# Products of ones at the start, first weights loaded in pieces, input squares as side work, and later places for the decays and the delta rule's sums, in a two-layer decoder trunk

## The chip, the core and the metric

One core of a Trainium2 chip runs the whole program. TensorE (PE, with its weight loads, PEld) multiplies, VectorE (DVE), ScalarE (ACT) and GpSimd (POOL) do the elementwise work, SyncE (SP) issues nearly all DMAs. The metric is the device time of one execution in microseconds (us); lower is better. The kernel before takes 2602.82 us, the median of three runs (2601.01 to 2603.27).

## The reference

The input is x, 256 positions of 2048 features in float32. Two layers follow one another; each adds a mixer, a cross-attention to a memory and a convolutional feed-forward block to the residual stream, each on an RMS-normalized input. The change lies in the mixer of the first (even) layer, which joins stick-breaking attention with a gated delta rule:

```python
def rmsnorm(x, g):
    y = xf * lax.rsqrt(jnp.mean(xf * xf, axis=-1, keepdims=True) + EPS)
    return (y * g.astype(jnp.float32)).astype(x.dtype)

def even_mixer(h, w_in, sconv_w, a_log, dt_bias, gdn_norm, w_out):
    sb_q, sb_k, sb_v, gdn_qkv, gdn_a, gdn_b, gdn_gate = split_cols(h @ w_in, [...])
    o_a = merge_heads(stick_breaking_attention(...))
    gq, gk, gv = split_cols(jax.nn.silu(causal_dwconv(gdn_qkv, sconv_w)), [...])
    log_decay = -jnp.exp(a_log) * jax.nn.softplus(gdn_a + dt_bias)
    beta = jax.nn.sigmoid(gdn_b)
    o_b = gated_delta_rule(l2norm(gq heads), l2norm(gk heads), gv heads, log_decay, beta)
    o_b = rmsnorm(o_b, gdn_norm) * jax.nn.silu(gdn_gate heads)
    return jnp.concatenate([o_a, o_b], axis=-1) @ w_out
```

There are eight delta-rule heads of width 128, worked in chunks of 64 positions.

## The kernel before

The residual stream stays on chip, features on partitions: X[0] to X[15], 128x256 each, loaded as eight tiles of two. Every float32 product is made of rounded parts: a weight slab (`raw`, 128x1024, 512 KB, five buffers) becomes `hi`, a rounded copy made by ACT (L229), and `lo`, the rest, made by DVE in two halves of 512 columns (L232); four pairs of such buffers are kept. An input tile X[k] becomes `xs`, 128x512, whose left half ACT writes (L218) and whose right half DVE writes (L219). One step of a matrix product (`mm_tile`) is then a product of `hi` with all 512 columns of `xs` (L261) and one of `lo` with the left 256 (L262), called a pair below; 16 pairs make one 128-wide output column block, `gemm`.

Work that is not a weight product, the attention chains and the delta rule, is written as generators. `Side` runs them between pairs: each pair is one tick, and `yield n` asks for at least n ticks before the generator goes on. A scheduler then moves single instructions a little; on each engine they execute strictly in the order that it leaves.

`even()` starts with the head of the program: for each k, X[k] is split into `xs`, multiplied with the first key weights of the delta rule (g0), and, from k = 4 on, with a narrow weight `wab` for the decays (`decay_products`, L437, two products into `pab`). GpSimd squares the odd X[k] and adds them up (L360, L364, `Norm.square`); the even ones are squared by ACT and added by DVE (L353, L354, `Norm.add`). The sums of both accumulators over partitions (L372) give the norm R, first wanted when the first three gemms of the delta rule are done. The generator `decays` turns `pab` into g, beta and their cumulated forms: two transposes on TensorE (L481), a chain of small ACT and DVE instructions, 12 ticks, then four small products (L499). For every two heads `delta_pair` normalizes keys and queries: squares (ACT writes the rounded square L566, GpSimd squares again L567 and subtracts L568), 8 ticks, sums over partitions on TensorE (L551), a reciprocal root (`rsqrt`, from L327) and the scaled `kq`, first for keys, then the same for queries, then 17 ticks before the products of `kq` (L585). Near its end the same is done for its output (ACT L713, L714, GpSimd L715), 8 ticks before the sums.

The weight slabs come from SP's queue in the order of use; the head's DMAs are in a list, `order`, that starts with the first X tile, the first slab of 512 KB, the second X tile and `wab`.

Of the kernel before, what the change touches and what calls it, by code (L numbers as in the profile page):

```python
# [10 lines left out]
F32 = mybir.dt.float32  # L11
F32R = mybir.dt.float32r
I32 = mybir.dt.int32
AF = mybir.ActivationFunctionType
# [133 lines left out]
def build(tc, nc, a):  # L148
# [23 lines left out]


    A.preload_act_table_set("natural_log_exp_and_others")
    cg = cp.tile([P, NCOL + 256], F32, name="cg")
# [3 lines left out]
    nc.scalar.dma_start(cg[:, 0:n0], a["cg"][:, 0:n0])  # L179
    order = [("x", 0), ("w", 0), ("x", 1), ("ab", 0), ("x", 2), ("x", 3), ("x", 4), ("w", 1), ("x", 5), ("x", 6), ("x", 7), ("q", 0), ("cg", 0), ("q", 1)]  # L180
    early = {}
    for what, j in order:
        if what == "x":
            nc.sync.dma_start(XT[j], a["x"][:, 2 * j:2 * j + 2])
        elif what == "cg":
            nc.sync.dma_start(cg[:, n0:], a["cg"][:, n0:])
        else:
            early[what, j] = load(a["wab"] if what == "ab" else a["w"][2 * OFF["ev_gq" if what == "q" else "ev_gk"] + j])
# [15 lines left out]
    def acc(name="a"):  # L204
        return pa.tile([P, 512], F32, name="ps_" + name, tag=name)
# [4 lines left out]
    def f32(ap):  # L210
        return ap.bitcast(F32)
# [12 lines left out]
    def part(raw):  # L224

        n = raw.shape[-1]
        hi = wp.tile([P, 1024], F32R, name="hi", bufs=4)
        lo = wp.tile([P, 1024], F32R, name="lo", bufs=4)
        A.copy(hi[:, 0:n], raw)  # L229
        for h in range(2):  # L230
            s = slice(h * n // 2, (h + 1) * n // 2)
            V.tensor_tensor(out=lo[:, s], in0=raw[:, s], in1=f32(hi[:, s]), op=ALU.subtract)  # L232
        return hi, lo

    cache = {}
# [190 lines left out]
    def even():  # L426
# [12 lines left out]
        for k in range(KD):  # L439
            first.feed(k, False)  # L440
            if k == 0:
                cache[OFF["ev_gk"], 0] = part(early["w", 0])
            if k == 2:
                wab = [e(f"wab{i}", (P, 512), 2, F32R, "kq0") for i in range(2)]
                A.copy(wab[0], early["ab", 0])
                V.tensor_tensor(out=wab[1], in0=early["ab", 0], in1=f32(wab[0]), op=ALU.subtract)
            if k == 7:
                cache[OFF["ev_gk"], 1] = part(early["w", 1])
            mm_tile(g0, [(OFF["ev_gk"], k, k)], xs, first=k == 0, last=k == KD - 1)
            if k >= 4:  # L450
                decay_products(k - 4)
            if k % 2:
                nm.square(X[k], G)
        for k in range(KD - 4, KD):
            decay_products(k)
        for k in range(0, KD, 2):
            nm.add(X[k], V)
            if k % 8 == 0:
                cache[OFF["ev_gq"], k // 8] = part(early["q", k // 8])
        mix, vts = [None] * 16, [None] * 2  # L460
# [12 lines left out]
        def decays():  # L473
            nc.sync.dma_start(cev, a["cev"][:, 0:3 * P])
            nc.sync.dma_start(cst, a["cev"][:, 3 * P:10 * P])
            nc.sync.dma_start(strict, a["iev"])
            y = evac(pab, 32)
            times(y[0:32], y[0:32], nm.R[0:32])
            ab = acc()
            for t in range(2):  # L480
# [13 lines left out]
            V.tensor_scalar(out=nbt, in0=bt, scalar1=-1.0, scalar2=None, op0=ALU.mult)  # L494
            yield 12
            g2 = g.rearrange("p t h -> p (t h)")
# [47 lines left out]

        def squares():
            return tmp("sq", bufs=2), e("sqs", (P, 2, S), 2, F32R, "sbs")

# [6 lines left out]
        def delta_pair(h0, kq0s, vs, sgts):  # L554
# [5 lines left out]
            vec = lambda n: e(n, (P, 2, P), 2)  # L560
            kq = [e("kq", (P, 2, 2, P), 2) for _ in two]
            for q in range(2):
                sps = []
                for i in two:
                    sq, sp = squares()
                    A.activation(sp[:, 0], kq0s[i][:, q], AF.Square)  # L566
                    G.tensor_tensor(out=sq, in0=kq0s[i][:, q], in1=kq0s[i][:, q], op=ALU.mult)  # L567
                    G.tensor_tensor(out=sp[:, 1], in0=sq, in1=f32(sp[:, 0]), op=ALU.subtract)  # L568
                    sps.append(sp)
                yield 8  # L570
                for i in two:
                    ps = sum_squares(sps[i])
                    r = rsqrt(ps, 256, 1.0).rearrange("p (t n) -> p t n", t=2)
                    z = kq0s[i][:, q].rearrange("p (t n) -> p t n", t=2)
                    V.scalar_tensor_tensor(out=kq[i][:, :, q], in0=z, scalar=P ** -0.5 if q else 1.0, in1=r, op0=ALU.mult, op1=ALU.mult)
            yield 17

# [103 lines left out]
            for c in range(4):  # L681
# [27 lines left out]
                yield 4  # L709
            sps = []  # L710
            for i in two:
                sq, sp = squares()
                A.activation(sq, po[:, i * 256:i * 256 + 256], AF.Square)  # L713
                A.copy(sp[:, 0], sq)  # L714
                G.tensor_tensor(out=sp[:, 1], in0=sq, in1=f32(sp[:, 0]), op=ALU.subtract)  # L715
                sps.append(sp)
            yield 8
            for i in two:
# [640 lines left out]
```

## Time and profile before

| what | value |
|---|---|
| median of three runs | 2602.82 us |
| the profiled execution's own time | 2601.66 us |
| its span, first to last instruction | 2599.9 us |
| TensorE busy | 2562.2 us (99%) |
| VectorE busy | 1983.2 us (76%) |
| ScalarE busy | 1480.6 us (57%) |
| GpSimd busy | 197.5 us (8%) |
| mean granted TensorE clock | 0.998 |

All times inside the program count from the start of the span. A bracket behind an instruction names how long its engine sat idle before it and what released it. Ends of TensorE products are modelled, so that a busy share of 99% does not mean full throughput; starts are what to compare.

### The profile page before, as it was taken

To read this page: it belongs to the slowest core of one execution; us is meant where nothing else is said; L and a number is where in the kernel's file an instruction comes from. 1 tells how busy PE (TensorE), PEld (TensorE's weight loads), DVE (VectorE), ACT (ScalarE), POOL (GpSimd) and SP (SyncE) were. 2 spreads that over 40 slices of the span, in tenths; PEclk is the share of its full clock that TensorE was granted. 3 is DMA by queue.
4 is the path that set the end of the run, shared out by engine and by line. 5 is a ranking of instruction groups with operands and counts; after the bars stand their busy time and mean duration, and the time that the engine had idled before them with its cause. 6 is when DMAs were issued, how large, how long until landed. Compare 5 with 4: busy or idle time off the path is not lost.

```text
span 2599.9 us, 41291 instructions
## 1 busy us (share of the span) xinstructions
PE 2562.2 (99%) x15183; PEld 2227.8 (86%) x15183; DVE 1983.2 (76%) x4045; ACT 1480.6 (57%) x2496; POOL 197.5 (8%) x267
## 2 busy tenths in 40 slices
PE   8999999999999999999999999999999999999997
PEld 6887888888888888888888888888988888888886
DVE  7888866877877767767777777886877777777766
ACT  6777655646655545545456555754655545545544
POOL 2111100201000000000011012120200000000001
PEclk9999999999999999999999999999999999999999
DMA  6333435654555555555555544365555555555563
GB/s 219 130 131 114 138 123 174 213 181 154 197 189 192 188 190 188 188 187 186 188 190 183 191 155 167 130 211 170 171 189 191 188 194 187 187 188 185 187 194 122
DMA packets 127404, 458.08 MB, mean 176 GB/s; under 512 B 14272, under 2 KB 14912, under 8 KB 127200
## 3 DMA queue, kind: packets, MB, share of 16 engines
q1 hardware_dynamic: 125856, 453.59, 52.5%
q8 instruction: 119, 1.95, 0.3%
q10 hardware_dynamic: 1344, 1.84, 0.2%
q14 instruction: 85, 0.70, 0.1%
HBM read 453.28 MB, written 2.10 MB: 175 GB/s over the span
## 4 chain that ended last, share of the span: by engine, by line
PE 91%; DVE 5%; ACT 2%; issue 1%; DMA 0%; POOL 0%; SPq 0%; DVEq 0%; ACTq 0%
PE g L261 53%; PE g L262 27%; DVE lo L232 2%; PE g L310 2%; PE g L313 2%; PE g L311 2%; DVE xs L219 1%; ACT hi L229 1%; PE ps_a L645 1%; DVE cv L521 0%; DVE X L400 0%; PE ps_a L1148 0%; PE ps_a L652 0%; PE ps_a L1113 0%; PE ps_a L585 0%
## 5 line engine op out<-in xcount | busy, mean ns | idle before, releaser
L232 DVE TENSOR_TENSOR lo<-raw,hi 128x512 fp32r<-128x512 f32 x1696 | 1176.0, 708 | 481.5 <-ACT hi L229 468.4
L261 PE MATMUL g<-xs,hi 128*128 128x512 f32 x4112 | 1462.3, 399 | 10.0 <-ACT hi L229 7.3
L229 ACT CAST hi<-raw 128x1024 fp32r<-128x1024 f32 (+1 forms) x848 | 889.4, 1050 | 831.8 <-PE g L261 534.0
L262 PE MATMUL g<-xs,lo 128*128 128x256 f32 x4112 | 1155.5, 281 | 3.8 <-DVE lo L232 3.8
L261 PEld LDWEIGHTS g<-xs,hi 128*128 128x128 f32 x4112 | 773.0, 188 | 193.4 <-ACT hi L229 7.3
L262 PEld LDWEIGHTS g<-xs,lo 128*128 128x128 f32 x4112 | 777.5, 189 | 6.6 <-DVE lo L232 5.3
L261 PE MATMUL g<-hid,hi 128*128 128x512 f32 x1397 | 484.6, 392 | 0.0
L262 PE MATMUL g<-hid,lo 128*128 128x256 f32 x1397 | 390.5, 280 | 0.0
L261 PEld LDWEIGHTS g<-hid,hi 128*128 128x128 f32 x1397 | 262.2, 188 | 58.0
L262 PEld LDWEIGHTS g<-hid,lo 128*128 128x128 f32 x1397 | 262.3, 188 | 0.0
L354 POOL TENSOR_TENSOR sqacc<-sqacc,sq 128x256 f32<-128x256 f32 x125 | 110.7, 889 | 1960.0 <-ACT sq L353 1954.8
L261 PE MATMUL g<-mix,hi 128*128 128x512 f32 x508 | 178.6, 394 | 0.0
L1176 DVE SCALAR_TENSOR_TENSOR fc<-y,cg,fc 128x255 f32<-128x255 f32 x352 | 168.2, 478 | 0.1
L262 PE MATMUL g<-mix,lo 128*128 128x256 f32 x508 | 142.1, 280 | 0.0
L321 DVE TENSOR_TENSOR y<-g,t 128x256 f32<-128x256 f32 x286 | 119.2, 418 | 6.4 <-ACT t L319 6.0
L400 DVE TENSOR_TENSOR X<-g,X 128x256 f32<-128x256 f32 x192 | 80.3, 419 | 47.8 <-PE g L262 41.6
L261 PEld LDWEIGHTS g<-mix,hi 128*128 128x128 f32 x508 | 95.2, 187 | 22.6
L1174 ACT ACTIVATE fc<-y,cg 128x256 f32<-128x256 f32 x176 | 105.4, 600 | 2.3 <-DVE y L1172 2.2
L319 ACT COPY t<-g 128x256 f32<-128x256 f32 x286 | 103.2, 362 | 5.9 <-PE g L262 5.9
L262 PEld LDWEIGHTS g<-mix,lo 128*128 128x128 f32 x508 | 95.2, 187 | 0.0
L1172 DVE TENSOR_TENSOR y<-y,R 128x256 f32<-128x256 f32 x176 | 73.7, 420 | 0.1
L218 ACT ACTIVATE xs<-X,cg 128x256 fp32r<-128x256 f32 x96 | 47.4, 506 | 40.6 <-DVE X L402 26.2
(356 smaller groups left out, 2312.7 us busy)
## 6 DMA issues: line engine op xcount, KB each, us to landing
raw<-w SPq DMA_DIRECT2D x846, 512.0 KB, 3.3
raw<-mem SPq DMA_DIRECT2D x8, 512.0 KB, 3.4
X<-x SPq DMA_DIRECT2D x8, 256.0 KB, 5.7
out<-xg SPq DMA_DIRECT2D x4, 256.0 KB, 2.3
out<-xg ACTq DMA_DIRECT2D x4, 256.0 KB, 2.4
raw<-w SPq DMA_DIRECT2D x2, 384.0 KB, 6.0
cg<-cg SPq DMA_DIRECT2D x1, 599.5 KB, 7.5
cst<-cev SPq DMA_DIRECT2D x1, 448.0 KB, 5.0
```

The costliest lines, as they stand in the source:

```text
L229: A.copy(hi[:, 0:n], raw)
L232: V.tensor_tensor(out=lo[:, s], in0=raw[:, s], in1=f32(hi[:, s]), op=ALU.subtract)
L261: T.matmul(ps[0:m, 0:512], lhsT=hi[:, w], rhs=xs[k], start=first and q == 0, stop=False)
L262: T.matmul(ps[0:m, 0:256], lhsT=lo[:, w], rhs=xs[k][:, 0:256], start=False, stop=last and q == n - 1)
L310: T.matmul(ps[t], lhsT=xh, rhs=hi[:, w], start=k == 0, stop=False)
L319: A.copy(t[0:m], ps[0:m, 256:512])
L321: V.tensor_tensor(out=y[0:m], in0=ps[0:m, 0:256], in1=t[0:m], op=ALU.add)
L354: eng.tensor_tensor(out=self.acc[eng], in0=self.acc[eng], in1=q, op=ALU.add)
L400: V.tensor_tensor(out=X[n], in0=ps[:, 0:256], in1=X[n], op=ALU.add)
L1172: V.tensor_tensor(out=y, in0=y, in1=R, op=ALU.mult)
L1174: A.activation(c, y, AF.Identity, scale=col(f"fc{l}", n * 3 + 2), bias=col(f"fb{l}", n))
L1176: V.scalar_tensor_tensor(out=c[:, s:], in0=y[:, 0:S - s], scalar=col(f"fc{l}", n * 3 + 2 - s), in1=c[:, s:], op0=ALU.mult, op1=ALU.add)
```

## The change

At the start, six products of a tile of ones with itself are issued on TensorE, into a PSUM tile that nothing reads. The first slab is loaded as two DMAs of 256 KB, the second of them behind X tile 2, and is split in three pieces (columns 0 to 255 at k = 0, 256 to 511 at k = 1, the rest at k = 3). The decay products follow from k = 3 on instead of 4. GpSimd no longer squares X in the head; all 16 squares are made by ACT, in a generator (`squares_of_input`) that runs beside the next gemms, and every third is added by GpSimd, the others by DVE. The split of the first query slabs no longer waits in the text for the squares. `decays` writes its sum into a tile of its own and waits 40 ticks before it multiplies with R, 8 more before the transposes, and 24 instead of 12 before the four small products. In `delta_pair` ACT makes the square and its rounded copy and GpSimd only subtracts, for all three uses; keys' and queries' squares stand 6 ticks apart, 6 ticks before the sums of the keys; 4 ticks lie between the two kinds of sums and 14 behind them; the output's sums come 12 ticks behind its squares.

```diff
+    warm = xp.tile([P, S], F32, name="warm", tag="xs", bufs=16)
+    V.memset(warm, 1.0)
+    idle = pa.tile([P, 512], F32, name="ps_a", tag="a")
+    for i in range(6):
+        T.matmul(idle[:, 0:256], lhsT=warm[:, 0:P], rhs=warm, start=i == 0, stop=i == 5)
...
-    order = [("x", 0), ("w", 0), ("x", 1), ("ab", 0), ("x", 2), ("x", 3), ("x", 4), ("w", 1), ...]
+    order = [("x", 0), ("w", 0, 0), ("x", 1), ("ab", 0), ("x", 2), ("w", 0, 1), ("x", 3), ("x", 4), ("w", 1), ...]
...
         for k in range(KD):
             first.feed(k, False)
             if k == 0:
-                cache[OFF["ev_gk"], 0] = part(early["w", 0])
+                hi, lo = cache[OFF["ev_gk"], 0] = parts()
+            if k in (0, 1, 3):
+                c = {0: slice(0, 256), 1: slice(256, 512), 3: slice(512, 1024)}[k]
+                A.copy(hi[:, c], w0[:, c])
+                low(hi, lo, w0, c)
...
-            if k >= 4:
-                decay_products(k - 4)
-            if k % 2:
-                nm.square(X[k], G)
-        for k in range(KD - 4, KD):
+            if k >= 3:
+                decay_products(k - 3)
+        for k in range(KD - 3, KD):
             decay_products(k)
-        for k in range(0, KD, 2):
-            nm.add(X[k], V)
-            if k % 8 == 0:
-                cache[OFF["ev_gq"], k // 8] = part(early["q", k // 8])
+        for j in range(2):
+            cache[OFF["ev_gq"], j] = part(early["q", j])
+
+        def squares_of_input():
+            for k in range(KD):
+                nm.add(X[k], G if k % 3 == 2 else V)
+                if k % 2:
+                    yield 1
+        side.spawn(squares_of_input())
...
-            y = evac(pab, 32)
+            y = e("yab", (P, S), 4, tag="st")
+            A.copy(y[0:32], pab[0:32, 256:512])
+            V.tensor_tensor(out=y[0:32], in0=pab[0:32, 0:256], in1=y[0:32], op=ALU.add)
+            yield 40
             times(y[0:32], y[0:32], nm.R[0:32])
+            yield 8
...
-            yield 12
+            yield 24
...
-        def squares():
-            return tmp("sq", bufs=2), e("sqs", (P, 2, S), 2, F32R, "sbs")
+        def squares_of(x):
+
+            sq, sp = tmp("sq", bufs=2), e("sqs", (P, 2, S), 4, F32R, "sqs")
+            A.activation(sq, x, AF.Square)
+            A.copy(sp[:, 0], sq)
+            G.tensor_tensor(out=sp[:, 1], in0=sq, in1=f32(sp[:, 0]), op=ALU.subtract)
+            return sp
...
+            sps = []
             for q in range(2):
-                sps = []
+                sps.append([squares_of(kq0s[i][:, q]) for i in two])
+                yield 6
+            for q in range(2):
                 for i in two:
-                    sq, sp = squares()
-                    A.activation(sp[:, 0], kq0s[i][:, q], AF.Square)
-                    G.tensor_tensor(out=sq, in0=kq0s[i][:, q], in1=kq0s[i][:, q], op=ALU.mult)
-                    G.tensor_tensor(out=sp[:, 1], in0=sq, in1=f32(sp[:, 0]), op=ALU.subtract)
-                    sps.append(sp)
-                yield 8
-                for i in two:
-                    ps = sum_squares(sps[i])
+                    ps = sum_squares(sps[q][i])
...
-            yield 17
+                yield 14 if q else 4
...
-            yield 8
+            sps = [squares_of(po[:, i * 256:i * 256 + 256]) for i in two]
+            yield 12
```

The order of the instructions on three engines, at three places. On VectorE, the start of its list; `xs` with a number is the split of the X tile with the number behind the arrow, two per X tile, `lo` belongs to the first slab until its 1024 columns are done and then to the second. Before:

```order
L219 SCALAR_TENSOR_TENSOR xs_111<-X_75,cg,xs_111 128x256
L219 SCALAR_TENSOR_TENSOR xs_121<-X_75,cg,xs_121 128x256
L232 TENSOR_TENSOR lo<-raw,hi 128x512 x2
L219 SCALAR_TENSOR_TENSOR xs_128<-X_76,cg,xs_128 128x256
L446 TENSOR_TENSOR wab_132<-raw,wab_131 128x512
L219 SCALAR_TENSOR_TENSOR xs_137<-X_76,cg,xs_137 128x256
L219 SCALAR_TENSOR_TENSOR xs_145<-X_77,cg,xs_145 128x256
```

Now:

```order
L175 MEMSET warm 128x256
L370 TENSOR_TENSOR sqacc<-sqacc,sq 128x256
L249 TENSOR_TENSOR lo<-raw,hi 128x256
L231 SCALAR_TENSOR_TENSOR xs_121<-X_84,cg,xs_121 128x256
L231 SCALAR_TENSOR_TENSOR xs_130<-X_84,cg,xs_130 128x256
L249 TENSOR_TENSOR lo<-raw,hi 128x256
L231 SCALAR_TENSOR_TENSOR xs_137<-X_85,cg,xs_137 128x256
L466 TENSOR_TENSOR wab_141<-raw,wab_140 128x512
L231 SCALAR_TENSOR_TENSOR xs_146<-X_85,cg,xs_146 128x256
L231 SCALAR_TENSOR_TENSOR xs_155<-X_86,cg,xs_155 128x256
L231 SCALAR_TENSOR_TENSOR xs_162<-X_86,cg,xs_162 128x256
L249 TENSOR_TENSOR lo<-raw,hi 128x512
```

One add of squares moved ahead of the first `xs` (ACT squares X[0] and X[1] ahead of its first `xs` too), and the first slab's `lo` is spread. Up to the last `xs` of the head, VectorE's list has 16 `xs`, 2 `lo` of 256 columns, 3 `lo` of 512, 1 `wab` and 3 adds now, and 16 `xs`, 4 `lo` of 512, 1 `wab` and 2 adds before.

On TensorE, the place of the transposes of the decays. Before, 72 pairs from the program's start lie ahead of it:

```order
L261 MATMUL g<-xs_169,hi 128x512
L481 MATMUL ps_a<-cg,y 128x32 x2
L262 MATMUL g<-xs_169,lo 128x256
L261 MATMUL g<-xs_184,hi 128x512
L262 MATMUL g<-xs_184,lo 128x256
```

Now 97 lie ahead:

```order
L277 MATMUL g<-xs_121,hi 128x512
L278 MATMUL g<-xs_121,lo 128x256
L508 MATMUL ps_a<-cg,yab 128x32 x2
L277 MATMUL g<-xs_130,hi 128x512
L278 MATMUL g<-xs_130,lo 128x256
```

The four small products behind them moved from behind 87 pairs to behind 121, so that 24 pairs instead of 15 lie between the two; both still stand ahead of the first sums of the delta rule (137 pairs before, 141 now).

On GpSimd, the first two heads' norms (`kq` with a number is the unnormalized key and query of one head; the rows up to `qg`). Before:

```order
L527 TENSOR_TENSOR kq_385<-cv,sg 128x256
L567 TENSOR_TENSOR sq<-kq_385 128x256
L527 TENSOR_TENSOR kq_385<-cv,sg 128x256
L568 TENSOR_TENSOR sqs<-sq,sqs 128x256
L527 TENSOR_TENSOR vd<-cv,sg 128x256
L567 TENSOR_TENSOR sq<-kq_552 128x256
L567 TENSOR_TENSOR sq<-kq_385 128x256
L568 TENSOR_TENSOR sqs<-sq,sqs 128x256
L567 TENSOR_TENSOR sq<-kq_552 128x256
L568 TENSOR_TENSOR sqs<-sq,sqs 128x256 x2
L600 TENSOR_TENSOR qg<-kq,qg 128x256 x2
```

Now:

```order
L554 TENSOR_TENSOR kq_398<-cv,sg 128x256
L577 TENSOR_TENSOR sqs<-sq,sqs 128x256
L554 TENSOR_TENSOR kq_398<-cv,sg 128x256
L554 TENSOR_TENSOR vd<-cv,sg 128x256
L577 TENSOR_TENSOR sqs<-sq,sqs 128x256 x3
L628 TENSOR_TENSOR qg<-kq,qg 128x256 x2
```

GpSimd's list lost one of its two instructions for each square of `kq`, 16 in the four pairs of heads, and its 15 instructions on X in the head became four adds.

## Rows read from the trace of the kernel before

**Rows 1.** The page's first lines: the span, then busy time, share of the span and instructions of each engine.

```profile
span 2599.9 us, 41291 instructions
PE 2562.2 (99%) x15183; PEld 2227.8 (86%) x15183; DVE 1983.2 (76%) x4045; ACT 1480.6 (57%) x2496; POOL 197.5 (8%) x267
```

**Rows 2.** Busy time by stretch: the stretch in us, its length, busy time (and instructions) of PE, PEld, DVE, ACT, POOL, then the granted clock, the DMA share and GB/s.

```profile
0.00:10.00 10.00, 2.02 (x4) 1.00 (x4) 3.61 (x5) 6.30 (x12) 4.07 (x11) 1.00 0.80 276
10.00:20.00 10.00, 7.82 (x25) 5.00 (x26) 9.90 (x13) 6.69 (x15) 8.32 (x11) 1.00 0.86 336
20.00:30.00 10.00, 10.00 (x58) 7.75 (x58) 9.43 (x21) 5.41 (x10) 0.00 (x0) 1.00 0.68 227
50.00:100.00 50.00, 47.20 (x263) 40.30 (x263) 46.91 (x112) 37.50 (x94) 10.27 (x12) 0.97 0.42 137
200.00:250.00 50.00, 45.30 (x315) 38.78 (x315) 47.90 (x112) 40.23 (x98) 10.52 (x12) 1.00 0.32 107
2000.00:2500.00 500.00, 500.00 (x2860) 437.11 (x2859) 372.98 (x751) 259.02 (x365) 0.00 (x0) 1.00 0.57 188
2500.00:2600.00 100.00, 86.40 (x507) 75.90 (x505) 65.09 (x118) 43.56 (x64) 13.62 (x16) 0.95 0.44 148
```

**Rows 3.** Whom TensorE waited for over the whole span: the waiting product, the releaser, us in total, times, the longest.

```profile
PE g L261 <- ACT hi L229: 7.3, 1, 7.3
PE g L262 <- DVE lo L232: 3.8, 3, 2.1
PE ps_a L551 <- POOL sqs L568: 3.8, 6, 1.1
PE g L261 <- DVE xs L219: 2.7, 4, 0.8
PE ps_a L551 <- DVE rs_v L327: 1.8, 1, 1.8
PE ps_a L499 <- DVE gd L492: 1.6, 1, 1.6
PE ps_a L607 <- ACT qg L596: 0.6, 1, 0.6
...
PE ps_a L481 <- DVE y L408: 0.5, 1, 0.5
PE ps_a L585 <- DVE kq L575: 0.5, 2, 0.3
```

**Rows 4.** The timeline of the head, all engines: start, us, engine, line, operation, tiles, count of merged instructions, and in brackets the idle time before and its releaser.

```profile
0.73 0.56 POOL L658 MEMSET U<- 128x256 f32 x2 [0.29 <-POOLq L1350]
...
4.89 0.42 ACT L350 ACTIVATE sqacc<-X 128x256 f32<-128x256 f32 x1 [2.87 <-DMA X<-x]
...
7.29 0.80 PE L261 MATMUL g<-xs,hi 128*128 128x512 f32 x1 [7.29 <-ACT hi L229]
...
11.18 5.70 DVE L219 SCALAR_TENSOR_TENSOR xs<-X,cg,xs 128x256 fp32r<-128x256 f32 x7
...
13.95 0.63 PE L261 MATMUL g<-xs,hi 128*128 128x512 f32 x1
...
17.42 0.39 PE L261 MATMUL g<-xs,hi 128*128 128x512 f32 x1
...
18.31 0.79 POOL L364 TENSOR_TENSOR sqacc<-sqacc,rs_q 128x256 f32<-128x256 f32 x1
...
19.71 0.39 PE L262 MATMUL g<-xs,lo 128*128 128x256 f32 x1 [1.55 <-DVE lo L232]
...
20.18 2.45 DVE L219 SCALAR_TENSOR_TENSOR xs<-X,cg,xs 128x256 fp32r<-128x256 f32 x6
...
22.89 1.28 DVE L232 TENSOR_TENSOR lo<-raw,hi 128x512 fp32r<-128x512 f32 x2
...
24.47 1.92 PE L437 MATMUL g<-xs,wab 128*32 128x512 f32 x10
...
26.22 0.40 PE L261 MATMUL g<-xs,hi 128*128 128x512 f32 x1
...
26.58 0.40 PE L261 MATMUL g<-xs,hi 128*128 128x512 f32 x1
```

**Rows 5.** TensorE's timeline at the sums of the input's squares: the products with ones, then what follows them. Two float32 products of 256 columns are four records.

```profile
37.54 1.02 PE L372 MATMUL ps_a<-sqacc,cg 128*128 128x256 f32 x4
38.40 0.95 PE L375 MATMUL ps_a<-cg,sqacc 128*128 128x1 f32 x8
```

**Rows 6.** TensorE's timeline at the decays.

```profile
48.32 0.30 PE L481 MATMUL ps_a<-cg,y 32*128 32x32 f32 x2 [0.51 <-DVE y L408]
...
55.75 0.40 PE L499 MATMUL ps_a<-gd,cst 128*128 128x16 f32 x2 [1.64 <-DVE gd L492]
```

**Rows 7.** Busy time by stretch behind the decays, columns as in Rows 2.

```profile
58.00:60.00 2.00, 2.00 (x8) 1.71 (x8) 2.00 (x7) 1.13 (x6) 0.86 (x1) 0.50 0.59 217
60.00:62.00 2.00, 2.00 (x10) 1.72 (x9) 1.80 (x5) 0.36 (x1) 0.00 (x0) 0.67 0.83 262
```

**Rows 8.** GpSimd's groups between 40 and 300 us: line, operation, tiles, shapes, count, busy us, mean ns, then its idle time before them and its releasers.

```profile
L568 POOL TENSOR_TENSOR sqs<-sq,sqs 128x256 fp32r<-128x256 f32 x16 | 15.6, 986 | 13.5 <-ACT sqs L566 13.5
L567 POOL TENSOR_TENSOR sq<-kq 128x256 f32<-128x256 f32 x16 | 14.5, 917 | 12.0 <-DVE kq L527 11.6
```

**Rows 9.** ScalarE's group of squares in the same stretch, columns as in Rows 8.

```profile
L566 ACT ACTIVATE sqs<-kq 128x256 fp32r<-128x256 f32 x16 | 6.4, 407 | 0.0
```

More of the change, by code (lines that the diff above doesn't have):

```diff
@@ L179, in build @@
     nc.scalar.dma_start(cg[:, 0:n0], a["cg"][:, 0:n0])
-    order = [("x", 0), ("w", 0), ("x", 1), ("ab", 0), ("x", 2), ("x", 3), ("x", 4), ("w", 1), ("x", 5), ("x", 6), ("x", 7), ("q", 0), ("cg", 0), ("q", 1)]
+    order = [("x", 0), ("w", 0, 0), ("x", 1), ("ab", 0), ("x", 2), ("w", 0, 1), ("x", 3), ("x", 4), ("w", 1), ("x", 5), ("x", 6), ("x", 7), ("q", 0), ("cg", 0), ("q", 1)]
     early = {}
-    for what, j in order:
-        if what == "x":
+    w0 = wp.tile([P, 1024], F32, name="raw", bufs=5)
+    early["w", 0] = w0
+    for what, j, *c in order:
+        if c:
+            c = slice(c[0] * 512, c[0] * 512 + 512)
+            nc.sync.dma_start(w0[:, c], a["w"][2 * OFF["ev_gk"]][:, c])
+        elif what == "x":
             nc.sync.dma_start(XT[j], a["x"][:, 2 * j:2 * j + 2])
@@ L226, in part, with parts, low @@
         n = raw.shape[-1]
-        hi = wp.tile([P, 1024], F32R, name="hi", bufs=4)
-        lo = wp.tile([P, 1024], F32R, name="lo", bufs=4)
+        hi, lo = parts()
         A.copy(hi[:, 0:n], raw)
         for h in range(2):
-            s = slice(h * n // 2, (h + 1) * n // 2)
-            V.tensor_tensor(out=lo[:, s], in0=raw[:, s], in1=f32(hi[:, s]), op=ALU.subtract)
+            low(hi, lo, raw, slice(h * n // 2, (h + 1) * n // 2))
         return hi, lo
+    def parts():
+        return [wp.tile([P, 1024], F32R, name=n, bufs=4) for n in ("hi", "lo")]
+    def low(hi, lo, raw, s):
+        V.tensor_tensor(out=lo[:, s], in0=raw[:, s], in1=f32(hi[:, s]), op=ALU.subtract)
     cache = {}
@@ L709, in delta_pair @@
                 yield 4
[L710 to L716, printed above, removed]
-            yield 8
+            sps = [squares_of(po[:, i * 256:i * 256 + 256]) for i in two]
+            yield 12
             for i in two:
```

## The prediction

> **What bounds the kernel now.** I read the totals first [rows 1]: TensorE is busy 2562.2 of 2599.9 us, so 37.7 us of idle time, and whatever runs at half clock, is all that a reordering can win. The busy time by stretch says where it lies [rows 2]: from 2000 to 2500 us TensorE is busy for 500.00 of 500, so the long feed-forward blocks have nothing to give; the first 10 us hold 7.98 idle, the next 10 hold 2.18, 50 to 100 holds 2.80, 200 to 250 holds 4.70, and the last 100 us hold 13.60, which no edit touches. The same rows show the engine behind it: VectorE is busy for 9.90 of 10 in the second stretch and for 46.91 and 47.90 of 50 in the other two. Third, the list of waits [rows 3] names the releasers. All but the tail's waits belong to the head (L261 behind hi and xs), to the decays (L481, L499) or to the delta rule (L551, L585, L607, and one lo of 2.1 us). Last, the head's timeline [rows 4], where the reader should see two things. While GpSimd squares X (until 18.31 + 0.79), seven xs of VectorE take 5.70 us, 0.81 each; after it, six take 2.45, 0.41 each. [...]
>
> **The change, part by part.** The sum is made against the profiled execution, 2601.66 us with a span of 2599.9; it lies 1.16 under the median of 2602.82.
>
> *The head.* What ends it is the last xs and the decay products behind it; the next gemm starts at 26.22 [rows 4]. VectorE's list now holds, from its first add to the last xs, 16 xs and 3 adds at 0.41 (7.8 us), two lo of 256 columns, which lie between 0.32 and 0.41 (half of a 512-column lo, and a 256-column xs; I take 0.4, nearest in width: 0.8), and three lo and one wab of 512 columns at 1.28 / 2 = 0.64 (2.6): 11.2 us, at the speed without GpSimd, whose four adds come behind. ACT squares X[0] and X[1] from 4.89, so VectorE starts at about 5.7 and ends at 16.9. TensorE follows with one pair (0.36, from 26.22 to 26.58) and eight decay products (ten took 1.92, so 1.5): 18.7 instead of 26.2, 7.5 us earlier. That is for full clock. The phase holds 16 pairs and 32 decay products, 5.8 + 6.1 = 11.9 us of work at full clock; if the clock rose at 17 as before, 10.1 us from the first product (5.7 + 3 x 0.41 = 6.9, against 7.29) would do 5.05 of it and the rest end at 23.8, 2.4 us earlier. So the gain lies between 2.4 and 7.5.
>
> The ones decide between these. A memset like them takes 0.28, so they start at about 1.0; two products with ones take 38.40 - 37.54 = 0.86 [rows 5], hence 0.86 each at half clock, and six end at about 6.2. TensorE is then busy for 5 us without a gap and idles for 0.7, far less than the 1.55 us at 19.71, after which products still ran at full clock. I take the upper end less 1.0 for a new wait: the query slabs' lo now share VectorE with ten adds of squares and four of GpSimd, and the nearest row for such a wait is that 1.55. **Head: -6.5.** The decay products' step from 4 to 3 and the piecewise DMA are inside this sum: SP issues one DMA more, and from X tile 3 on the same bytes lie ahead of each tile. The ones' own 5 us cost nothing, since TensorE waited until 7.29; that cover would be gone if they ran past 6.9.
>
> [...]
>
> *The decays.* [...] The transposes move behind 25 more pairs (9 us), and 24 instead of 15 pairs lie between them and the small products, 8.6 us instead of 5.4, so the chain has 3.2 us more against a wait of 1.64. Bounds 0 and -3.8; I take nearly all. **Decays: -3.5.** Late next would be the delta rule's first sums, 20 pairs on.
>
> *The delta rule.* GpSimd loses 16 squares, 14.5 us [rows 8]; ACT gains 16 casts, at about the 0.41 of its square [rows 9] 6.5 us over four pairs of heads, where it has 12.5 and 9.8 us free per 50 [rows 2]. Sums wait for GpSimd for 3.8 and for rs_v for 1.8; L607, L585 and the lo add 0.6, 0.5 and 2.1 [rows 3]: 8.8. The sums of the keys get 12 ticks instead of 8 behind their squares, the others 10 and 12 instead of 8, and each chain loses 0.92 us of GpSimd; I expect about 4 of the 5.6 back. VectorE, the full engine here, should gain by half of what GpSimd no longer does beside it, by the head's ratio of 0.81 to 0.41, but only where they met; I take 0.5 of the other 3.2. Against it, 14 instead of 17 ticks lie behind the last sums: 1 us less for a chain that was late at L585 twice by 0.3, so up to 2 us lost. Bounds -8.8 and +2. **Delta rule: -4.5.**
>
> Sum: -6.5 - 3.5 - 4.5 = -14.5: 2587.2 against the profiled execution, 2588.3 against the median. I give **2588**.
>
> **The rivals.** A run of this kernel can tell about 0.2% from no change, 5.2 us: faster means under 2597.6.
>
> *A. The ones do not lift the clock* (the change does not do what it says). For it: the rise came only after products ran with hardly a gap [rows 4], and the clock fell behind a stall of 1.64. Against: ones are products like others. Then the head gives its lower end, 2.4, the decays 3.5, and the delta rule, which starts with VectorE no further ahead, half, 2: 2602.8 - 7.9 = 2595. [...]
>
> *B. VectorE stays the bound from 50 to 300.* For it: 47.90 of 50. Against: TensorE's largest waits name GpSimd. The stalls then come back elsewhere, and the earlier start is eaten by the ten adds (4 us) and GpSimd's adds moved behind the head: 2600.
>
> *C. Slower: ACT becomes the bound.* The squares wait for two buffers that VectorE and GpSimd free, in ACT's queue ahead of the casts hi; TensorE waits behind them. [...] Against it: ACT is busy for only 37.50 and 40.23 of 50 [rows 2].
>
> **How the numbers follow.** Forecast 0.63, A 0.24, B 0.10, C 0.03. Faster takes the forecast and nearly all of A (0.22), no change the rest of A and 0.08 of B with its neighbours: faster 0.86, same 0.11, slower 0.03. The low end has all three terms at their best, 7.5 + 3.8 + 8.8, from the profiled execution: 2581. The high end takes in A with a weaker delta rule, 2597; B, C and the far ends, some 0.18, stay outside.
>
> **What would show it.** Right: products of 0.39 us soon after 7 us, xs of 0.41 on VectorE throughout the head, the query gemm from about 19 us, no wait at the transposes and the small products, no granted clock of 0.50 around 50 us, and less than 2 us of waits of L551's successor. Wrong: products of 0.63 until 13 us or later (A); new waits behind lo in the query and value gemms or in 200 to 250 with VectorE full (B); waits behind hi with ACT near 50 of 50 (C).

## The result and the profile after

The changed kernel takes 2589.03 us, the median of four runs (2588.32 to 2590.20), beside 2603.03 for the kernel before in the same set of runs: a ratio of 0.9948, with a 95% interval of 0.9936 to 0.9960, so 13.5 us less (10 to 17). The forecast was 2588. The profiled execution took 2590.20 us, the longest of the four, with a span of 2588.4; against the profiled execution before (2601.66), it is 11.5 us shorter.

The page's line of busy time, share of the span and instructions of each engine and the busy time by stretch (columns as in [rows 2]) answer to [rows 1, 2]. Here and below, rows between those shown are left out:

```profile
PE 2560.0 (99%) x15195; PEld 2228.8 (86%) x15195; DVE 1972.0 (76%) x4050; ACT 1485.5 (57%) x2522; POOL 175.6 (7%) x240
```

```profile
10.00:20.00 10.00, 9.66 (x53) 6.74 (x52) 9.48 (x21) 8.99 (x24) 1.94 (x2) 1.00 1.02 404
50.00:100.00 50.00, 47.58 (x339) 41.27 (x340) 46.94 (x122) 41.25 (x108) 5.56 (x6) 0.97 0.43 140
200.00:250.00 50.00, 47.03 (x399) 39.61 (x398) 46.36 (x116) 39.53 (x100) 4.96 (x6) 1.00 0.36 119
```

The head is full now (9.66 of 10 in the second stretch, 7.82 before), but 50 to 100 us holds 2.42 of idle time, hardly less than the 2.80 before. The list of TensorE's waits says why; it answers to [rows 3]:

```profile
PE ps_a L583 <- DVE rs_v L343: 6.2, 4, 2.4
PE ps_a L583 <- ACT sg L433: 2.2, 3, 0.8
PE g L277 <- DVE xs L231: 2.1, 4, 0.8
PE ps_a L613 <- DVE kq L603: 2.0, 2, 1.0
```

The waits for hi, for GpSimd's sqs and for the decays' y and gd are gone. In their place the sums (L583) wait for rs_v and sg, and the products with kq (L613) for kq: 10.4 us in the delta rule. The head's timeline, which answers to [rows 4]:

```profile
1.19 5.01 PE L178 MATMUL ps_a<-warm 128*128 128x256 f32 x12 [1.19 <-DVE warm L175]
6.45 0.50 PE L277 MATMUL g<-xs,hi 128*128 128x512 f32 x1 [0.25 <-DVE xs L231]
9.92 1.67 DVE L231 SCALAR_TENSOR_TENSOR xs<-X,cg,xs 128x256 fp32r<-128x256 f32 x4
14.17 2.96 DVE L231 SCALAR_TENSOR_TENSOR xs<-X,cg,xs 128x256 fp32r<-128x256 f32 x6
19.35 0.40 PE L277 MATMUL g<-xs,hi 128*128 128x512 f32 x1
```

Products of 512 columns take 0.50 us and less from the first on, xs takes 0.42, later 0.49 on average (one of those six, beside an add of GpSimd at 15.72, takes 0.98), and the query gemm starts at 19.35 instead of 26.22: 6.87 us earlier. What became of the delta rule's first sums is seen on TensorE and, beside it, on VectorE:

```profile
66.14 0.63 PE L583 MATMUL ps_a<-sqs,onesr 128*128 128x256 f32 x4
70.80 0.76 PE L583 MATMUL ps_a<-sqs,onesr 128*128 128x256 f32 x2 [2.39 <-DVE rs_v L343]
```

```profile
69.04 1.28 DVE L249 TENSOR_TENSOR lo<-raw,hi 128x512 fp32r<-128x512 f32 x2
70.25 0.41 DVE L343 TENSOR_SCALAR rs_v<-ps_a 128x256 f32<-128x256 f32 x1
73.19 0.41 DVE L343 TENSOR_SCALAR rs_v<-ps_a 128x256 f32<-128x256 f32 x1
```

Four sums want a PSUM tile each and there are three. The first is free when VectorE has read it as rs_v, in the instruction that starts at 70.25, although its products (66.14) ended before 67: lo, y and vd stand ahead of rs_v in VectorE's list. The fourth sum waits 2.39 us for that, and the clock falls as it did behind the decays before [rows 7]:

```profile
70.00:72.00 2.00, 1.20 (x4) 1.13 (x5) 1.14 (x4) 1.77 (x6) 0.00 (x0) 0.61 0.82 274
72.00:74.00 2.00, 2.00 (x8) 1.71 (x8) 2.00 (x7) 1.78 (x4) 0.00 (x0) 0.54 0.72 233
```

That is 2 x 0.39 + 2 x 0.46 = 1.70 us of TensorE's full speed lost. Some 0.2 of it cost nothing: the granted clock is 0.62 from 70.4 to 70.5 and 0.50 from there on, while the fourth sum, which starts at 70.80, was still waiting. A product of 512 columns takes 0.63 us at this 0.50 (71.36 to 73.28) and 0.39 at 1.00 (74.26).

### The profile page after: what moved, and what is told of

Read it like the earlier page. It is cut to its first block, busy times and chain, and to the rows that moved or that the text cites. A ratio compares the mean times of both kernels' runs of the same rounds, so it can differ in the third digit from the quotient of the medians.

```text
span 2588.4 us, 41299 instructions
## 1 busy us (share of the span) xinstructions
PE 2560.0 (99%) x15195; PEld 2228.8 (86%) x15195; DVE 1972.0 (76%) x4050; ACT 1485.5 (57%) x2522; POOL 175.6 (7%) x240
## 4 chain that ended last, share of the span: by engine, by line
PE 92%; DVE 5%; ACT 2%; issue 1%; POOL 0%; DMA 0%; SPq 0%; DVEq 0%; ACTq 0%; POOLq 0%
PE g L277 53%; PE g L278 27%; PE g L326 2%; PE g L329 2%; PE g L327 2%; DVE lo L249 2%; DVE xs L231 1%; PE ps_a L673 1%; DVE cv L548 1%; DVE X L416 0%; ACT hi L240 0%; PE ps_a L1170 0%; PE ps_a L613 0%; PE ps_a L680 0%; PE ps_a L1135 0%
## 5 line engine op out<-in xcount | busy, mean ns | idle before, releaser
L249 DVE TENSOR_TENSOR lo<-raw,hi 128x512 fp32r<-128x512 f32 (+1 forms) x1697 | 1172.2, 705 | 477.0 <-ACT hi L240 462.7
```

## The experiments

The theory after the comparison: the head's 6.9 us are kept; the decays' gain and the old waits of the sums were exchanged for new waits of the sums, since VectorE comes late there. The rival: each term is worth what it was forecast at. Each kernel was run in turn with the kernel before; the medians of before in the sets lie between 2601.91 and 2603.03, so differences of about 1 us between kernels of different sets are not told apart. Below, "longer" compares medians with the changed kernel's 2589.03, where no other kernel is named.

| Kernel | median us (range, runs) | ratio to before (95%) |
|---|---|---|
| changed | 2589.03 (2588.32 to 2590.20, 4) | 0.9948 (0.9936 to 0.9960) |
| changed, no ones | 2589.47 (2588.99 to 2590.48, 5) | 0.9953 (0.9940 to 0.9965) |
| before, with ones | 2603.09 (2601.81 to 2606.09, 11) | 1.0004 (0.9995 to 1.0013) |
| changed, GpSimd squares X in the head | 2593.90 (2592.50 to 2595.38, 6) | 0.9969 (0.9957 to 0.9980) |
| changed, old decays | 2589.72 (2588.94 to 2591.87, 5) | 0.9955 (0.9942 to 0.9969) |
| changed, old sums | 2595.59 (2595.16 to 2596.96, 11) | 0.9978 (0.9969 to 0.9986) |
| changed, squares by ACT and GpSimd | 2595.31 (2593.70 to 2595.82, 7) | 0.9970 (0.9959 to 0.9982) |
| changed, fewer squares of X | 2589.99 (2588.21 to 2590.25, 5) | 0.9949 (0.9937 to 0.9962) |
| changed, one PSUM tile for two sums | 2589.23 (2588.05 to 2589.52, 5) | 0.9947 (0.9934 to 0.9959) |
| the same, 6 ticks more | 2595.17 (2592.16 to 2597.19, 9) | 0.9972 (0.9962 to 0.9982) |
| changed, own tiles for each chain | 2589.06 (2587.34 to 2590.94, 5) | 0.9949 (0.9936 to 0.9961) |
| one PSUM tile and own tiles | 2589.59 (2587.10 to 2592.10, 5) | 0.9952 (0.9939 to 0.9964) |
| one PSUM tile, one chain for two heads | 2598.81 (2597.52 to 2599.79, 11) | 0.9986 (0.9977 to 0.9995) |

**The ones, taken out and put in alone.**

```diff
-    warm = xp.tile([P, S], F32, name="warm", tag="xs", bufs=16)
-    V.memset(warm, 1.0)
-    idle = pa.tile([P, 512], F32, name="ps_a", tag="a")
-    for i in range(6):
-        T.matmul(idle[:, 0:256], lhsT=warm[:, 0:P], rhs=warm, start=i == 0, stop=i == 5)
```

> The changed kernel without its products of ones. Theory (the ones lift TensorE's clock before the operands come, and the head needs it): in the profile, products of 512 columns take 0.63 us until well past 7 us, the query gemm starts at 21.5 to 24 us instead of 19.35, and the whole is 2 to 4.5 us longer than the changed kernel (2591 to 2593.5). Rival (VectorE's list paces the head whatever the clock): the query gemm starts at 19.4 within 0.5, and the whole stays within 1 us of 2589.0. The decays and the delta rule are untouched; stalls there should stand as in the changed kernel.

TensorE's timeline without the ones:

```profile
9.68 0.61 PE L270 MATMUL g<-xs,hi 128*128 128x512 f32 x1
10.74 0.40 PE L270 MATMUL g<-xs,hi 128*128 128x512 f32 x1
20.41 0.40 PE L270 MATMUL g<-xs,hi 128*128 128x512 f32 x1
```

The products take 0.61 us up to 9.68 and 0.40 from 10.74; since 5.78 they had run with one gap of 0.17. In the head the granted clock reads 1.00 throughout, and the clock is read off these times, beside the 0.63 at 0.50 and 0.39 at 1.00 above: it is up by 10.74, where a product of the kernel before still took 0.63 at 13.95 [rows 4]. (GpSimd is gone from beside VectorE and the first slab comes in pieces; which of the two does it was not taken apart.) The query gemm starts 1.06 us later, which is nearer to the rival, and the whole is 0.44 longer, which is no difference. Then the same lines were added to the kernel before:

> The kernel before with the products of ones alone added. The prediction on record has the clock decide 5.1 us of the head: by it, products of 512 columns take 0.39 us from about 7 us and the query gemm starts some 2 to 5 us before 26.22. Theory after the run without the ones (the clock rises by itself once products come densely, and VectorE's xs, slowed beside GpSimd, pace the head): full clock early, yet the query gemm starts at 25 to 26.3 us, and the whole is within 1.2 us of the kernel before (2601.9).

VectorE's seven xs and TensorE's first product of the query gemm:

```profile
9.35 5.72 DVE L226 SCALAR_TENSOR_TENSOR xs<-X,cg,xs 128x256 fp32r<-128x256 f32 x7
24.65 0.40 PE L268 MATMUL g<-xs,hi 128*128 128x512 f32 x1
```

With the clock up from 7 us (a product of 512 columns takes 0.39 at 7.22) and xs still at 0.82, the query gemm starts 1.57 us earlier, a little more than expected, and the whole gains nothing (0.6 us longer than before). The clock is not what held the head: alone it brings 1.57 of the 6.87 us. In the profiled execution even these were lost again, at 222 us, where the granted clock is 0.51 to 224 and 0.64 to 226 (1.70 us), against 1.00 in the kernel before (last section).

**GpSimd's squares back in the head.**

```diff
+            if k % 2:
+                nm.square(X[k], G)
...
-            for k in range(KD):
-                nm.add(X[k], G if k % 3 == 2 else V)
-                if k % 2:
-                    yield 1
+            for k in range(0, KD, 2):
+                nm.add(X[k], V)
+                yield 1
```

> The changed kernel, but GpSimd squares the odd X tiles inside the head's loop, as before, and VectorE alone adds the even ones as side work. Theory (GpSimd beside VectorE doubles the time of VectorE's xs): xs at about 0.8 us until GpSimd is through, against 0.49 for the six around 14 us in the changed kernel; the query gemm starts at 22.5 to 25 us instead of 19.35, the whole 3 to 6 us longer (2592 to 2595). Rival (the ones alone brought the head's gain, VectorE had room): start at 19.4 to 20.5, the whole within 1.5 us of 2589.0.

```profile
12.53 3.33 DVE L231 SCALAR_TENSOR_TENSOR xs<-X,cg,xs 128x256 fp32r<-128x256 f32 x4
23.99 0.40 PE L277 MATMUL g<-xs,hi 128*128 128x512 f32 x1
```

xs takes 0.83 again, with the ones in place; the query gemm starts 4.64 us later and the whole is 4.9 us longer. The theory holds: this is most of the head's gain. Of the 6.87 us at the query gemm, GpSimd's squares make 4.64 and the ones 1.06 when taken out; some 1.2 are left, among them what the first slab in pieces does, which was not taken out.

**The decays back in their old places.**

```diff
-            y = e("yab", (P, S), 4, tag="st")
-            A.copy(y[0:32], pab[0:32, 256:512])
-            V.tensor_tensor(out=y[0:32], in0=pab[0:32, 0:256], in1=y[0:32], op=ALU.add)
-            yield 40
+            y = evac(pab, 32)
             times(y[0:32], y[0:32], nm.R[0:32])
-            yield 8
...
-            yield 24
+            yield 12
```

> The changed kernel with the decays' steps where they were: the copy of the sums by the general helper, the transposes right behind it, the small products 12 ticks later. Theory (two waits and the half clock behind the second are what the moved steps saved): waits of 0.4 to 0.6 at the transposes and of 1.4 to 1.9 at the small products come back some 7 us earlier than they stood before, a granted clock of 0.50 behind the second, and the whole is 3.5 to 4.3 us longer (2592.5 to 2593.3). Rival (with the head out of the way VectorE is less full, so the chain is in time anyway): no wait over 0.5 us, no fall of the clock, the whole within 1 us of 2589.0.

Among TensorE's waits (whole span, in us, times, longest):

```profile
PE ps_a L579 <- DVE rs_v L343: 4.7, 4, 1.3
PE ps_a L522 <- DVE gd L515: 1.2, 1, 1.2
PE ps_a L504 <- DVE y L424: 1.0, 1, 1.0
PE ps_a L579 <- ACT sg L433: 0.8, 1, 0.8
```

Both waits are back, 1.2 and 1.0, with no fall of the clock behind either (1.00 from 30 to 70). But TensorE now comes to the first sums later, so these wait 2.9 us less than in the changed kernel (4.7 + 0.8 against 6.2 + 2.2), and the clock stays up there too (1.00 from 70 to 100). The whole is 0.7 us longer, which is no difference: not the theory's number, and not for the rival's reason. What the decays' new places save is given back at the sums. (The profiled execution is the fastest of its five and the changed kernel's the slowest of its four, so their spans are not compared.)

**The delta rule's sums as before.** The functions are those of the change's diff, turned round, with 8, 8 and 17 ticks, and 8 for the outputs:

```diff
-                sps.append([squares_of(kq0s[i][:, q]) for i in two])
-                yield 6
...
+                    A.activation(sp[:, 0], kq0s[i][:, q], AF.Square)
+                    G.tensor_tensor(out=sq, in0=kq0s[i][:, q], in1=kq0s[i][:, q], op=ALU.mult)
+                    G.tensor_tensor(out=sp[:, 1], in0=sq, in1=f32(sp[:, 0]), op=ALU.subtract)
```

> The changed kernel with the delta rule's squares and sums as before: squares twice over on ACT and GpSimd, keys' sums 8 ticks behind their squares, queries' after them, 17 ticks to the next step. Prediction on record (the sums' new places are worth 4.5 us): the whole is 4 to 5 us longer, 2593 to 2594. Theory from the trace of the changed kernel (the waits for GpSimd, 3.8 us, went, and waits for rs_v, 6.2 us, came in their place): the whole within 1.5 us of 2589.0; waits of the sums for GpSimd of 3 to 4 us come back, waits for rs_v fall under 2.5 us. Whether the granted clock falls around 70 us decides some 1.7 us either way.

6.6 us longer. The reading from the trace alone was wrong, and the prediction's 4.5 was too little. The waits, however, did come back as that reading said:

```profile
PE ps_a L578 <- POOL sqs L595: 3.8, 6, 0.9
PE ps_a L578 <- ACT sqs L593: 2.5, 3, 1.8
PE g L278 <- DVE lo L249: 2.0, 1, 2.0
PE ps_a L578 <- DVE rs_v L343: 1.8, 1, 1.8
```

With 0.6 for qg they add up to 10.7, hardly more than the 10.4 of the changed kernel. The granted clock falls twice instead of once (0.60 and 0.55 from 74 to 78, 0.56 and 0.59 from 238 to 242; 1.7 us each), and the span is 5.4 us longer; 3.4 of it are neither in these waits nor in the clock and were not traced to a cause. Against the kernel before, the 145th pair starts 10.5 us earlier and the last one only 6.1: here the earlier start is lost in the delta rule. In the changed kernel it is 11.3 and 11.4. Comparing only before and after would have called the new sums worthless; without them, the head's and the decays' gain would have been half lost.

**Which part of it: the order or GpSimd's squares.** All of the change stays, ticks and order, but the squares of keys and queries are formed twice again:

```diff
-                sps.append([squares_of(kq0s[i][:, q]) for i in two])
+                sps.append([squares_by_both(kq0s[i][:, q]) for i in two])
...
+        def squares_by_both(x):
+            sq, sp = tmp("sq", bufs=2), e("sqs", (P, 2, S), 4, F32R, "sqs")
+            A.activation(sp[:, 0], x, AF.Square)
+            G.tensor_tensor(out=sq, in0=x, in1=x, op=ALU.mult)
+            G.tensor_tensor(out=sp[:, 1], in0=sq, in1=f32(sp[:, 0]), op=ALU.subtract)
+            return sp
```

> The changed kernel with its order and ticks, but the squares of keys and queries formed twice again, on ACT and on GpSimd, as before (16 squares more on GpSimd, 14.5 us, and 16 casts less on ACT). It splits what the old sums cost, 6.6 us. Theory (the order is what counts: in the changed kernel all four squares are issued 12 ticks ahead of the first sum): the waits for GpSimd stay under 1 us, and the whole is within 1.5 us of 2589.0. Rival (GpSimd's squares are what counts, by their own length and by what they take from VectorE beside them): waits for GpSimd of 2 us or more, rs_v later, the whole 3 to 6 us longer, 2592 to 2595.

6.3 us longer, where the old sums cost 6.6: most of their cost, and about the rival's time. (By the ratios to before it is 5.7 of 7.8, so up to some 2 us may belong to the order.) But TensorE waits for GpSimd not once; the list of its waits begins so:

```profile
PE ps_a L591 <- DVE rs_v L343: 8.3, 7, 3.1
PE g L278 <- DVE lo L249: 4.1, 4, 1.4
...
PE ps_a L656 <- DVE atf L635: 1.4, 2, 0.7
```

So the cost goes through VectorE. Its work beside GpSimd, first in the changed kernel, then in this one with GpSimd's rows below (start, duration):

```profile
62.66 0.69 DVE L249 TENSOR_TENSOR lo<-raw,hi 128x512 fp32r<-128x512 f32 x1 [0.18 <-ACT hi L240]
63.27 0.48 DVE L548 SCALAR_TENSOR_TENSOR cv<-y,cg,cv 128x255 f32<-128x255 f32 x1
```

```profile
63.52 1.13 DVE L249 TENSOR_TENSOR lo<-raw,hi 128x512 fp32r<-128x512 f32 x1
64.58 0.83 DVE L548 SCALAR_TENSOR_TENSOR cv<-y,cg,cv 128x255 f32<-128x255 f32 x1
62.32 1.79 POOL L585 TENSOR_TENSOR sqs<-sq,sqs 128x256 fp32r<-128x256 f32 x2
64.07 1.06 POOL L584 TENSOR_TENSOR sq<-kq 128x256 f32<-128x256 f32 x1
```

The same instructions take 1.13 and 0.83 instead of 0.69 and 0.48. The ends tell more: lo ends at 64.65, some 0.54 behind the end of GpSimd's subtracts (64.11), and cv at 65.41, 0.28 behind the end of its square (65.13). The changed kernel's trace has the same: of the instructions that take over 0.06 us more than the median of those with none of GpSimd's beside them, 28 xs and 8 cv end 0.28 to 0.29 us behind the end of an instruction of GpSimd, and 75 of 76 lo of 512 columns 0.54 to 0.55. That VectorE's instruction is held until GpSimd's has ended, and does not run more slowly, is the author's reading of these ends and was not tested. Over the span, VectorE's 4050 instructions take 1980.4 us here and 1972.0 in the changed kernel: 8.4 us for 16 squares of GpSimd of 0.94. TensorE's three waits of 13.8 us against 10.4, and a second fall of the clock (0.66 and 0.50 from 167 to 171, 1.7 us), make 5.1 of the 5.2 by which the span is longer.

**Is it VectorE's load before the sums?**

```diff
-                nm.add(X[k], G if k % 3 == 2 else V)
+                if k == 0 or k % 3 == 2:
+                    nm.add(X[k], G if k % 3 == 2 else V, 1.633)
```

> The changed kernel without ten of the sixteen input tiles in the sum of squares: the ten adds on VectorE and their squares on ACT are left out, and the other six squares are scaled up to keep the size. Theory (VectorE's list between 20 and 70 us is full, so what is added there comes out as the first pair's wait): rs_v of the first sum starts right behind its products instead of 3 us later, the wait of 2.39 at 70.80 and the clock's fall behind it vanish, the whole is 3 to 5 us shorter, 2584 to 2586. Rival (what stands directly ahead of rs_v in VectorE's order, lo and y of the running gemm, makes it late, whatever was added before): the wait stays between 1.5 and 2.4, the whole within 1.5 us of 2589.0.

```profile
PE ps_a L584 <- DVE rs_v L343: 5.9, 4, 2.0
```

The wait at the fourth sum stays, at 2.0 us, the mean granted clock is 0.997 (0.998 in the changed kernel), and the whole does not move: the rival's forecast came true. VectorE's ten adds of the input's squares cost nothing that can be measured. That what stands right ahead of rs_v in its list does cost is what is left, and was not tested by itself.

**Attempts to take the remaining waits away.** First, fewer PSUM tiles:

```diff
-            for i in range(2):
-                T.matmul(ps[:, 0:256], lhsT=onesr, rhs=sp[:, i], start=i == 0, stop=i == 1)
-            return ps
+            for j, sp in enumerate(sps):
+                for i in range(2):
+                    T.matmul(ps[:, j * 256:j * 256 + 256], lhsT=onesr, rhs=sp[:, i], start=i == 0, stop=i == 1)
+            return [ps[:, j * 256:j * 256 + 256] for j in two_]
```

> The changed kernel with the sums of both heads in one PSUM tile (columns 0 to 255 and 256 to 511), so that four sums need two of the three tiles instead of four. Theory (the waits of the sums for rs_v and sg, 8.4 us, and the fall of the clock at 70.42, 1.7, come from waiting for a tile): those waits fall under 1.5 us, no clock of 0.50 around 70 us, the whole 3 to 8 us shorter, 2581 to 2586. Rival (the chain from the sums over rs_v to kq on VectorE sets the pace): the products with kq wait in their place, 2.0 us in the changed kernel, 5 us or more here, and the whole is within 1.5 us of 2589.0.

```profile
PE ps_a L615 <- DVE kq L605: 9.8, 7, 2.9
```

The rival was right: no sum waits, and the products with kq wait 9.8 us instead. Behind the first of these, the clock is low from 80 to 87 (0.54, 0.50, 0.50 and 0.75 by steps of 2 us up to 88). Giving that chain more ticks (`yield 20 if q else 4`):

> As the kernel with one PSUM tile for both heads, and 20 ticks instead of 14 between the queries' sums and the products with kq. Theory (what is left behind the sums is the chain to kq, and six more pairs, 2.1 us, cover it): waits at the products with kq under 0.5 us, the whole 1 to 3 us under that kernel's. Rival (later steps of the delta rule, now 8 us later over four pairs of heads, find less work beside them): the same or up to 3 us longer, with new waits behind 300 us.

Worse than either: 5.9 us longer than with one tile alone. VectorE's list shows what fills the ticks:

```profile
77.11 0.42 DVE L343 TENSOR_SCALAR rs_v<-ps_a 128x256 f32<-128x256 f32 x1
77.44 2.49 DVE L249 TENSOR_TENSOR lo<-raw,hi 128x512 fp32r<-128x512 f32 x4
79.85 0.42 DVE L349 SCALAR_TENSOR_TENSOR rs_q<-rs_q,rs_v 128x256 f32<-128x256 f32 x1
```

Four lo of the gemm that the ticks brought forward stand between rs_v and rs_q, which starts 2.74 us behind rs_v. The waits for kq shrink only from 9.8 to 8.8 us, and 3.3 for lo are new. (The profiled execution is the fastest of nine, 3.0 us under their median; the rest of the difference is not shown by it.) Next, the four chains from rs_v to kq, which run one behind the other since rs_v and rs_y have one buffer each (rs_v at 70.25 and 73.19 above):

```diff
-                    r = rsqrt(ps, 256, 1.0).rearrange("p (t n) -> p t n", t=2)
+                    r = rsqrt(ps, 256, 1.0, own=e("sqs", (P, 2, S), 4, F32, "sqs")).rearrange("p (t n) -> p t n", t=2)
```

> The changed kernel, but each of the four chains from a sum to kq has tiles of its own for rs_v and rs_y (in the buffers that the squares no longer need), where all had one of each; the operations are the same. Theory (four chains of 3.5 to 3.9 us in series, because the next rs_v has to wait for the last one's tile, are what the sums and the products with kq wait for; not VectorE's load): rs_v of the second sum starts within 1.5 us of the first instead of about 3, the waits of the sums and of the products with kq, 10.4 us together, fall under 4, and the whole is 4 to 8 us shorter, 2581 to 2585. Rival (VectorE has too much to do here, in whatever order): lo is late instead, new waits at the gemm's second product of 3 us or more, the whole within 2 us of 2589.0.

```profile
PE ps_a L635 <- ACT qg L624: 3.2, 2, 1.6
PE ps_a L583 <- ACT mix L226: 2.7, 3, 0.9
PE ps_a L583 <- DVE sqs L343: 2.4, 1, 2.4
...
PE ps_a L583 <- ACT sg L433: 0.7, 1, 0.7
PE ps_a L613 <- DVE kq L603: 0.5, 1, 0.5
```

Of the 10.4 us of waits for rs_v, sg and kq 3.6 are left, but 5.9 for qg and mix, both on ACT, come in their place: 9.5 together, and the whole stays. The theory's waits went and its gain did not come; the rival's time is right, though lo is not late. (The profiled execution, 2587.34, is the fastest of five, and the clock does not fall in it: 1.00 in every 50 us from 50 to 350.) The last two:

> One PSUM tile for both heads and tiles of their own for each of the four chains. Theory (chains in series): what waits for a PSUM tile in the kernel with own tiles alone goes too; sums and products with kq wait for under 2 us together, the whole 2580 to 2584. Rival (VectorE's load): as with own tiles alone, within 1 us of that, with lo late.

2589.59: the same again. The waits are 7.8 us for kq and 3.2 for qg, and none for lo.

> The kernel with one PSUM tile for both heads, and one chain of 512 columns for both heads in place of two of 256 (with the inverse root's correction by three operations of VectorE, where ACT had squared once). Theory (chains in series): two chains of about 5 us instead of four of 3.7, waits at the products with kq 9.8 there, under 4 here, the whole 2581 to 2585. Rival (VectorE's load): VectorE does one operation of 512 columns more per chain; lo is late instead, the whole within 2 us of 2589.0 or above.

9.8 us longer. VectorE has about as much to do (242.7 us busy from 50 to 350 in 16 instructions fewer, against 247.9 in the changed kernel). The waits for kq, qg and atf are 15.2 us, and four falls of the clock lose some 8.5 (0.60 from 80 to 84, 0.57 from 152 to 156, 0.67 from 158 to 162 and 0.81 to 164, 0.57 from 230 to 238). Against the kernel with one PSUM tile, the waits for kq are alike (10.1 and 9.8); 5.1 us for qg and atf and 5.1 more of low clock come on top. The chain's results are not simply late: at the first two heads the first kq is done at 76.4 instead of 73.9 in the changed kernel, but the last at 80.5 instead of 85.9. Why the later steps then wait was not found. No version beats the changed kernel.

## Why the prediction came out right, and where it was wrong

**The time** was 1.0 us off (2589.03 against 2588.0), but the three terms do not stand as written. That the sum came so near is in part luck: the decays were taken 2.8 us too high and the delta rule 2.1 too low.

| Term | forecast | measured by taking it out |
|---|---|---|
| Head | 6.5 | 4.9 for GpSimd's squares, 0.4 for the ones |
| Decays | 3.5 | 0.7, not told from nothing |
| Delta rule | 4.5 | 6.6 |

These are differences of medians. By the ratios to before they are 5.5 and 1.3, 1.8 and 7.8, since before's median was 1.1 us lower in that set.

**Head: mechanism half right.** VectorE's list at the speed without GpSimd gave 18.7 for the query gemm; it was 19.35. VectorE began 0.6 us earlier than assumed and took 0.8 longer (0.5 of it at the one xs beside GpSimd's add, 0.3 idle before a lo), so that xs ended at 17.13 instead of 16.9; and one pair and two decay products still stood ahead of the last pair, 0.5 us. The step that failed is "the ones decide between these": the lower end of 2.4 is the author's estimate with half clock up to 17 us, as the products' 0.63 at 13.95 and 0.39 at 17.42 had it before [rows 4]. No run shows it: even without the ones the products take 0.40 from 10.74, after one gap of 0.17 since 5.78 (that the few gaps did this was not tested). So ones and no ones are 1.06 us apart in the head, and rival A's price, 2595, was too high by far: without any ones it is 2589.47.

**Decays: the step that failed is the size, taken as if it were kept.** The waits of 0.51 and 1.64 [rows 6] and the low clock behind them (0.50 and 0.67 from 58 to 62 us, which loses 2 x 0.50 + 2 x 0.33 = 1.66 [rows 7]) are gone, as forecast. They add up to the 3.8 of which the forecast took 3.5; no run shows 3.8 or 3.5 as the decays' gain: the old places put back cost 0.7. But the text itself said what would be late next, the first sums, and then costed that at nothing. The same fall of the clock is at 70 us now, behind a wait of 2.39.

**Delta rule: the size is of the right order, but its main reason failed.** The waits for GpSimd went, as forecast, but the step "I expect about 4 of the 5.6 back" did not come true, nor did "less than 2 us of waits" at L551's successor: those waits grew from 5.6 to 8.4 us. The gain is in the half-sentence that VectorE should gain by what GpSimd no longer does beside it, which was priced at 0.5 us: it is 8.4 us of VectorE's time and, with the squares alone put back, 6.3 us of the whole. [Rows 4] held the ratio (0.81 to 0.41) and [rows 8] the length (14.5 us of squares).

**Rivals.** B's mechanism, stalls that come back elsewhere and eat the earlier start, is what the changed kernel with the old sums does (10.5 us earlier, then 6.1); the new sums prevent most of it. C did not happen: ACT is busy for 41.25 and 39.53 of 50, and no product waits for hi.

**Left open.** In six variants, with the waits at the sums, at kq, at qg or at the decays, the whole lies between 2589.0 and 2590.0. Each wait taken away came back at another step. Why the whole stays there was not found.

## What to carry to other kernels

Price an engine's work also by what it takes from its neighbour: here 1 us of GpSimd's squares cost VectorE 0.56 us (8.4 of 15.0), and no wait for GpSimd showed it. Terms of a sum add up only as long as what they gain is not awaited by the same late engine further on; take one part out of the finished change to see what it is worth, since the difference of two traces credits it to the wrong part. And a stall may cost more than its length, 2.39 us of waiting and some 1.5 of low clock behind it at the fourth sum, so ask where the next such stall will be.

## What the runs showed of the hardware

The clock does not fall behind every stall of one length. In the kernel before, a sum waits 1.79 us at 222.75 and the clock stays up; in the kernel before with ones, the same sum waits 1.79 us at 221.37 and it falls. The sum's row and the granted clock (third column from the end) of before, then with ones:

```profile
222.75 0.48 PE L551 MATMUL ps_a<-sqs,onesr 128*128 128x256 f32 x2 [1.79 <-DVE rs_v L327]
222.00:224.00 2.00, 1.25 (x8) 1.20 (x9) 2.00 (x6) 1.16 (x4) 0.00 (x0) 1.00 0.12 47
```

```profile
221.37 0.48 PE L558 MATMUL ps_a<-sqs,onesr 128*128 128x256 f32 x2 [1.79 <-DVE rs_v L334]
222.00:224.00 2.00, 2.00 (x8) 1.68 (x7) 2.00 (x7) 0.59 (x2) 0.00 (x0) 0.51 0.00 0
```

Executions of one kernel lie up to some 5 us apart here while TensorE's work is the same, and the mean granted clock goes with the time: of 15 executions of the kernel before in one set, the five at 0.998 took 2600.91 to 2601.35 us, the six at 0.997 2602.54 to 2602.90 and the four at 0.996 2602.33 to 2604.66. That a fall more or less, some 1.7 us, makes these steps is likely and was not shown, since only the profiled executions tell where the clock fell.
